# Differential attention scores: the low-part term of the keys over 128 rows in place of 64, with keys doubled by a DMA

## The chip, the cores and the metric

The kernel runs on one core of a Trainium2 chip. The metric is the time of one execution on the device in microseconds, as the median of several runs. The engines are TensorE (PE for its matmuls, PEld for its weight loads), VectorE (DVE), ScalarE (ACT), GpSimd (POOL) and SyncE (SP, whose queue issues the DMAs here).

## The reference

One block of a transformer on a sequence of 512 tokens of width 2048, in float32. Branch A is differential attention with 8 heads: each head has two queries and two keys of 64 columns, two softmaxes, and one value of 128 columns. Branch B is grouped-query attention with 8 heads of 128 columns.

```
h = rmsnorm(x, norm_g); proj = h @ w_in            # (512, 10752)
qa, ka, va, za, qb, kb, vb, zb, ga, gb = split(proj)
# branch A, per head, with 1-D rope on q and k:
s1 = q1 @ k1.T * 64 ** -0.5;  s2 = q2 @ k2.T * 64 ** -0.5
p  = softmax(s1) - lam * softmax(s2)
oa = rmsnorm(p @ v, subln_g) * (1 - lam_init)
ya = (oa * silu(za)) @ w_out_a
# branch B: rmsnorm of q and k, axial rope, softmax, 4 query heads to a key head
yb = (ob * silu(zb)) @ w_out_b
x  = x + (sigmoid(ga) * ya + sigmoid(gb) * yb) @ w_o
out = rmsnorm(x, final_g)
```

## The kernel before, in words

Each float32 product is made of float32r products: an operand is split into a rounded high part and the remaining low part, and hi·hi, lo·hi and hi·lo are added up in PSUM. The split is `hi_lo` (lines 102 to 104): ScalarE casts the high part, VectorE subtracts it.

The kernel has three stages. First the norm of x and most of the input projection, with all gates, in Strassen's form (line 234). Then the sixteen heads of attention, between whose steps TensorE takes pieces of plain products, called fills (`stream_steps`, line 175): what is left of the input projection, then the output projection of branch B, and at the end that of branch A. Then the rest of the output projections, the merge and the final norm.

The order of the heads is the list `HEADS` (B0 B1 A0 B2 B3 B4 B5 A1 A2 B6 B7 A3 A4 A5 A6 A7), and `FILLS` gives for each head how many fills follow its first two score tiles, its last two, and the turning of its probabilities. On TensorE that order is the order of the program (`manual_schedule`); on the other engines, and in SP's queue of DMAs, a scheduler orders the instructions by its own estimates. So the order of those changes with the program.

The loop over heads issues for head n: `scores(0)`, `scores(1)`, the attention product of the head before (`finish`, line 618), fills, `scores(2)`, `scores(3)`, then `turn` of head n+1 (its operands for the scores), `prepare` of head n+2 (loads and rope), `norm` of the head before (lines 685 and 686), fills, `turn_p` (16 transposes of the probabilities, line 605), fills.

A head of branch A holds its two halves on the partitions: rows 0 to 63 of the turned queries and keys are the first half, rows 64 to 127 the second. `turn` makes for each half a tile `qs` of 128 rows, [q_hi; q_lo], and a tile `kh` of 128 rows, [k_hi; k_hi]: four casts of 64 rows on ScalarE (line 643), as a half has to reach both halves of the partitions. The low part `kl` is one tile of 128 rows for both halves (lines 637 and 638). A score tile of one half is then two matmuls of 512 columns, line 660 over all 128 rows (q_hi·k_hi + q_lo·k_hi) and line 661 over the 64 rows of its half (q_hi·k_lo):

```
for half in range(2):
    qs, kh, src = self.ops[half]
    sp = aux()
    nc.tensor.matmul(out=sp, lhsT=qs[:, sl], rhs=kh, start=True, stop=False)
    nc.tensor.matmul(out=sp, lhsT=qs[src, sl], rhs=self.kl[src], start=False, stop=True)
```

A call of `scores(i)` does this for two halves, and two calls stand together, so that TensorE takes blocks of eight matmuls, lines 660 and 661 in turn: 2 blocks for each of 8 heads, 16 in all. The softmax after each tile is a maximum on VectorE (`nmax`, line 576), an exponential on ScalarE (line 579), a scaling on ScalarE (line 668) and the combination of both halves into `p` on VectorE (line 669). Branch B's score tiles are three matmuls over 128 rows each (line 735).

Of the kernel before, what the change touches and what calls it, by code (L numbers as in the profile page):

```python
# [17 lines left out]
P = 128  # L18
# [12 lines left out]
# blocks of 128 columns of the intermediate that keeps the branches' projections  # L31
# [6 lines left out]
# which of them take Strassen's form, four at a time, and which are taken plainly beside the heads  # L38
# [3 lines left out]
# heads of branch B whose scalings ScalarE does  # L42
WIDE = "0125"
# halves of tiles of w whose products go before the first head and between the steps of each
# [5 lines left out]
def hybrid_block_kernel(  # L50
# [5 lines left out]
    """Every float32 product runs as three single-pass float32r products: each operand is split  # L56
    exactly into a rounded high part and the remaining low part (hi*hi + lo*hi + hi*lo). All but
    the keys and queries of branch A and the branches' output projections take Winograd's form of Strassen's product (seven eighths of the work)."""
# [4 lines left out]
    # the eight banks of PSUM, shared between accumulators and the rest  # L63
# [33 lines left out]
    def rsqrt_pool(dst, ss, mul, add, n):  # L97
        """dst = (ss * mul + add) ** -0.5 on a few columns."""
        nc.gpsimd.tensor_scalar(out=dst, in0=ss, scalar1=mul, scalar2=add, op0=ALU.mult, op1=ALU.add)
        nc.gpsimd.tensor_tensor(out=dst, in0=dst, in1=neg_half[:, :n], op=ALU.pow)  # L100
# [12 lines left out]
    def split_w(raw, free=None):  # L113
        """free: a raw slot from which the parts' places may be taken, with its next."""
# [9 lines left out]
    def load_w(w, pieces, kc, step):  # L124
        """Rows kc * 128.. of some columns of w, [128, step, columns]."""
# [11 lines left out]
    def stream_steps(w, pieces, nk, natural, act, done, order=None, early=None, halves=False):  # L137
        """Products with some columns of w (512 or 256, made of `pieces` of columns), over nk
        contraction tiles, in banks of PSUM [128, 512].
        natural: tokens by columns, act(k, t).T @ w; done(first token tile, bank), the token tiles of  # L140
        a bank side by side. Else columns by tokens, w[:, c].T @ act(k); done(c, bank). halves: so, but
        one half of the tokens after the other, act(k, half).
        A generator, of two steps for each tile of w."""
# [4 lines left out]
        # of a product: its bank, its place there, the columns of w, what act takes, first and last of the bank  # L148
# [12 lines left out]
        # two tiles of w take turns where the halves of the tokens do  # L161
# [24 lines left out]
    def strassen(w, c_left, c_right, act, natural, tmp, done, tail=None, before={}):  # L186
        """Winograd's form of Strassen's product over the whole contraction (2048 rows of w, its
        upper and lower 1024) for 256 + 256 columns of w and the two halves of the tokens.
        act: the seven sums of quarters of the activations, each [128, 8, 256], split hi/lo.
        tmp(): a [128, 2, 256] tile; done(token half, column half, psum, sbuf): a result, the sum of  # L190
        the two, [128, 2, 256]. natural: rows of the results are tokens, else columns of w. tail:
        the first half of the tokens comes early and the last results by token tiles; tail(u, p5, t)
        takes what the results have before: both of the other half, its right one alone and the right one
        of the first half. before:
        what prepares a sum of act, by its name."""
# [79 lines left out]
        # the next group's quarters take the slots in the order in which they fall free  # L275
# [13 lines left out]
    # the halves of the width, [128, token half, contraction tile, 256], hi and lo  # L289
# [9 lines left out]
    def keep_cols(blocks, t0, nt, v):  # L299
        """Token tiles t0.. of some 128-column blocks of the projection, [128, nt, columns], to DRAM."""  # L300
        for i, b in enumerate(blocks):
            written[b] = written.get(b, 0) + nt
            nc.sync.dma_start(out=pv[b, :, t0:t0 + nt, :], in_=v[:, :, i * P:(i + 1) * P])
# [10 lines left out]
    def plain_cols(blocks, place, **kw):  # L314
        """Blocks of 128 columns of the projection by tokens, as they come, kept in DRAM."""
# [9 lines left out]
    def plain_rows(blocks, place, **kw):  # L325
        """The same the other way: columns by tokens."""
# [12 lines left out]
    with tc.tile_pool(name="xs", bufs=1) as xs:  # L339
        # ---- h = rmsnorm(x), transposed: its quarters (halves of the tokens and of the width) and  # L340
        # ---- their sums; the first product needs the quarters alone
# [3 lines left out]
        with tc.tile_pool(name="xn", bufs=1) as xn:  # L345
            # the gain, by channels on the partitions
# [28 lines left out]
            def turned_in(kp):  # L375
                """Where the transposed quarters of two contraction tiles stay for a while, in the
                place of what they come from: [128, token half, tile, width half, 256]."""
# [50 lines left out]
            # ---- the other columns of branches A and B, kept in DRAM  # L428
# [9 lines left out]
            # the first ones go beside the last sums of quarters; results go where these were, the first  # L438
            # of them after a while in PSUM
# [639 lines left out]
```

## Time and profile before

| | |
|---|---|
| median of 3 runs | 1399.37 us (1399.13, 1399.37, 1401.01) |
| profiled execution | span 1399.1 us from its first to its last instruction; no other time is given for it, and the fastest run, 1399.13 us, is the same to the last digit |
| PE busy | 1375.2 us, 98% of the span |
| PEld, DVE, ACT, POOL busy | 1272.8, 1081.0, 720.0, 85.8 us |
| DMA | 200.02 MB, mean 143 GB/s |
| attention stage | from about 735 to 1143 us of the span |

In a timeline each row is the start in us, the length in us, the engine, the line, the operation and its output and inputs. Matmuls overlap: the length of one is from its start to its modelled end, so what one costs in a row of them is read from the starts, not from the lengths. In brackets stand the idle time before an instruction and what ended it. "64\*128 64x512" is a matmul over 64 rows with 512 columns. PEclk in a table of windows is the granted share of TensorE's full clock.

### The profile page before, as it was taken

How to read it: one execution, taken by the hardware profiler on the slowest of the kernel's cores; microseconds unless marked ns; L12 is line 12 of the kernel's file. 1: busy time of each engine (PE TensorE's matmuls, PEld its weight loads, DVE VectorE, ACT ScalarE, POOL GpSimd, SP SyncE). 2: the span in 40 equal slices, each digit the busy share in tenths (PEclk: the TensorE clock that was granted, in tenths of full speed). 3: DMA queues.
4: the chain of work that ended last, by engine and by line, in shares of the span. 5: the costliest groups of instructions: out<-in, count | busy, mean ns of one | idle time of the engine just before them, and what ended most of it. 6: DMA issues, size and time to landing. Idle time of an engine off the chain costs nothing.

```text
span 1399.1 us, 24056 instructions
## 1 busy us (share of the span) xinstructions
PE 1375.2 (98%) x9625; PEld 1272.8 (91%) x9625; DVE 1081.0 (77%) x1392; ACT 720.0 (51%) x1134; POOL 85.8 (6%) x94
## 2 busy tenths in 40 slices
PE   6999999999999999999999999999999999999997
PEld 5999999999999999999998798778777778899997
DVE  5967777777777877777758778677788867899986
ACT  7643334444444444444457667665766753444444
POOL 1000000000000000000021010000000010004322
PEclk9999999999999999999999999999999999999999
DMA  8245444544334344443366344435565336563333
GB/s 286 87 134 172 124 124 120 151 151 144 115 119 129 119 132 151 144 134 119 125 200 181 107 144 143 123 111 158 153 180 160 117 111 211 175 230 112 99 103 120
DMA packets 199183, 200.02 MB, mean 143 GB/s; under 512 B 10768, under 2 KB 174880, under 8 KB 198432
## 3 DMA queue, kind: packets, MB, share of 16 engines
q1 hardware_dynamic: 199072, 198.49, 45.7%
q8 instruction: 75, 1.23, 0.4%
q14 instruction: 36, 0.29, 0.1%
HBM read 165.68 MB, written 32.77 MB: 142 GB/s over the span
## 4 chain that ended last, share of the span: by engine, by line
PE 94%; DVE 2%; ACT 1%; issue 1%; DMA 0%; POOL 0%; SPq 0%; POOLq 0%; DVEq 0%; ACTq 0%
PE acc L234 55%; PE acc L175 28%; PE aux L618 3%; PE aux L605 2%; PE aux L661 2%; PE aux L660 2%; PE aux L735 2%; DVE w_lo L104 1%; DVE w_raw L209 1%; DMA xt<-in_x_dram 0%; PE aux L389 0%; PE aux L587 0%; ACT sq L366 0%; ACT w_hi L103 0%; PE aux L685 0%
## 5 line engine op out<-in xcount | busy, mean ns | idle before, releaser
L103 ACT CAST w_hi<-w_raw 128x1024 fp32r<-128x1024 f32 x351 | 368.5, 1050 | 517.0 <-PE acc L234 397.7
L104 DVE TENSOR_TENSOR w_lo<-w_raw,w_hi 128x1024 fp32r<-128x1024 f32 x351 | 434.5, 1239 | 166.2 <-ACT w_hi L103 163.6
L209 DVE TENSOR_TENSOR w_raw<-w_raw 128x1024 f32<-128x1024 f32 x160 | 200.0, 1250 | 2.4
L234 PE MATMUL acc<-a2l,w_hi 128*128 128x256 f32 x384 | 108.7, 283 | 0.0
L234 PE MATMUL acc<-a2h,w_hi 128*128 128x256 f32 x384 | 108.7, 283 | 0.0
L234 PE MATMUL acc<-a2h,w_lo 128*128 128x256 f32 x384 | 108.7, 283 | 0.0
L576 DVE TENSOR_REDUCE nmax<-aux 128x1 f32<-128x512 f32 x96 | 64.5, 687 | 17.5 <-PE aux L661 15.0
L234 PEld LDWEIGHTS acc<-a2h,w_hi 128*128 128x128 f32 x384 | 73.7, 192 | 0.0
L234 PEld LDWEIGHTS acc<-a2l,w_hi 128*128 128x128 f32 x384 | 73.7, 192 | 0.0
L234 PEld LDWEIGHTS acc<-a2h,w_lo 128*128 128x128 f32 x384 | 73.7, 192 | 0.0
L175 PE MATMUL acc<-a1h,w_hi 128*128 128x512 f32 (+1 forms) x160 | 56.4, 357 | 0.2 <-ACT a1h L393 0.2
L175 PE MATMUL acc<-a2h,w_hi 128*128 128x512 f32 (+1 forms) x160 | 55.5, 350 | 0.0
L175 PE MATMUL acc<-a2l,w_hi 128*128 128x512 f32 (+1 forms) x160 | 55.5, 348 | 0.0
L175 PE MATMUL acc<-a1h,w_lo 128*128 128x512 f32 (+1 forms) x160 | 55.4, 351 | 0.0
L175 PE MATMUL acc<-a2h,w_lo 128*128 128x512 f32 (+1 forms) x160 | 55.4, 347 | 0.0
L175 PE MATMUL acc<-a1l,w_hi 128*128 128x512 f32 (+1 forms) x160 | 55.2, 350 | 0.1
L234 PE MATMUL acc<-s1h,w_lo 128*128 128x256 f32 x192 | 54.3, 283 | 0.0
L234 PE MATMUL acc<-s4h,w_lo 128*128 128x256 f32 x192 | 54.3, 283 | 0.0
L234 PE MATMUL acc<-s1h,w_hi 128*128 128x256 f32 x192 | 54.3, 283 | 0.0
L234 PE MATMUL acc<-s1l,w_hi 128*128 128x256 f32 x192 | 54.3, 283 | 0.0
L234 PE MATMUL acc<-s2h,w_lo 128*128 128x256 f32 x192 | 54.3, 283 | 0.0
L234 PE MATMUL acc<-a1h,w_hi 128*128 128x256 f32 x192 | 54.3, 283 | 0.0
(326 smaller groups left out, 4376.9 us busy)
## 6 DMA issues: line engine op xcount, KB each, us to landing
w_raw<-in_w_in_dram SPq DMA_DIRECT2D x136, 512.0 KB, 3.5
w_raw<-in_w_in_dram SPq DMA_DIRECT2D x64, 256.0 KB, 3.6
w_raw<-in_w_o_dram SPq DMA_DIRECT2D x32, 512.0 KB, 4.0
gg<-kept SPq DMA_DIRECT2D x32, 256.0 KB, 2.5
w_raw<-in_w_out_b_dram SPq DMA_DIRECT2D x32, 256.0 KB, 3.2
rows<-gg SPq DMA_DIRECT2D x32, 256.0 KB, 3.1
w_raw<-in_w_out_a_dram SPq DMA_DIRECT2D x32, 256.0 KB, 3.3
cols<-pv SPq DMA_DIRECT2D x26, 256.0 KB, 2.9
```

Of the source, the lines that this page charges most:

```text
L103: nc.scalar.copy(out=hi, in_=src)
L104: nc.vector.tensor_tensor(out=lo, in0=src, in1=hi.bitcast(F32), op=ALU.subtract)
L175: nc.tensor.matmul(out=acc[b][:, place], lhsT=l, rhs=r, start=first and kc == order[0] and k == 0 and i == 0, stop=last and kc == order[-1 ...
L209: nc.vector.tensor_tensor(out=d, in0=u, in1=v, op=ALU.subtract)
L234: nc.tensor.matmul(out=ps[u] if by_row else ps[:, u, :], lhsT=l, rhs=r, start=n % (2 if by_row else 4) == 0 and k == 0 and i == 0, stop=n ...
L576: nc.vector.tensor_reduce(out=nmax, in_=sps, axis=AX.X, op=ALU.max, negate=True)
L605: nc.tensor.transpose(out=tp[:, i * P:(i + 1) * P], in_=self.p[i][:, j * P:(j + 1) * P], identity=ident)
L618: nc.tensor.matmul(out=o, lhsT=l, rhs=r, start=j == 0 and i == 0, stop=j == NT - 1 and i == 2)
L660: nc.tensor.matmul(out=sp, lhsT=qs[:, sl], rhs=kh, start=True, stop=False)
L661: nc.tensor.matmul(out=sp, lhsT=qs[src, sl], rhs=self.kl[src], start=False, stop=True)
L735: nc.tensor.matmul(out=sp, lhsT=l, rhs=r, start=n == 0, stop=n == 2)
```

## The change

Line 661's product runs over all 128 rows, [q_hi; q_lo] against [k_lo; k_lo], so each half gets a `kl` of its own with the low part on both halves of the partitions; the term q_lo·k_lo is added by it. The doubling moves from casts to DMAs: a new step `double()` copies each half of the roped keys twice, SBUF to SBUF, into a tile `kd` (4 DMAs of 64 rows and 128 KB for a head, 32 in all), and `turn` makes `kh` and `kl` from `kd` by `hi_lo`, 128 rows at a time. `double()` of head n+1 is called at the start of head n. `kn` goes, `kd` has four buffers (two tiles of two), `kl` now takes two buffers for a head. To make room, `y1` of the norm shares the place of `sqh`, and `bsq` of branch B's norm has a place of its own.

```
     class Head:
+        def double(self):
+            pass
...
     class HeadA(Head):
+        def double(self):
+            self.kd = [at.tile([P, S], F32, name="kd", tag="kd", bufs=2) for _ in range(2)]
+            for half in range(2):
+                for d in range(2):
+                    nc.sync.dma_start(out=self.kd[half][d * 64:d * 64 + 64], in_=self.k[half * 64:half * 64 + 64])
+
         def turn(self):
-            k, q = self.k, self.q
-            kl = at.tile([P, S], F32R, name="kl", tag="kl")
-            kh = [at.tile([P, S], F32R, name="kh", tag="kh") for _ in range(2)]
+            q = self.q
             self.ops = []
-            kn = at.tile([P, S], F32R, name="kn", tag="kn", bufs=1)
-            nc.scalar.copy(out=kn, in_=k)
-            nc.vector.tensor_tensor(out=kl, in0=k, in1=kn.bitcast(F32), op=ALU.subtract)
             for half in range(2):
                 src, oth = slice(half * 64, half * 64 + 64), slice(64 - half * 64, P - half * 64)
+                kh = at.tile([P, S], F32R, name="kh", tag="kh")
+                kl = at.tile([P, S], F32R, name="kl", tag="kl")
+                hi_lo(kh, kl, self.kd[half])
                 qs = at.tile([P, S], F32R, name="qs", tag="qs")
-                for d in (src, oth):
-                    nc.scalar.copy(out=kh[half][d], in_=k[src])
                 nc.scalar.mul(out=qs[src], in_=q[src], mul=0.125)
...
-                self.ops.append((qs, kh[half], src))
-            self.kl = kl
+                self.ops.append((qs, kh, kl))
...
-                qs, kh, src = self.ops[half]
+                qs, kh, kl = self.ops[half]
                 sp = aux()
                 nc.tensor.matmul(out=sp, lhsT=qs[:, sl], rhs=kh, start=True, stop=False)
-                nc.tensor.matmul(out=sp, lhsT=qs[src, sl], rhs=self.kl[src], start=False, stop=True)
+                nc.tensor.matmul(out=sp, lhsT=qs[:, sl], rhs=kl, start=False, stop=True)
...
-        sq = at.tile([P, P], F32, name="bsq", tag="y1", bufs=1)
+        sq = at.tile([P, P], F32, name="bsq", tag="bsq", bufs=1)
...
-            y1 = at.tile([P, S], F32, name="y1", tag="y1", bufs=1)
+            y1 = at.tile([P, S], F32, name="y1", tag="sqh", bufs=1)
...
         heads[1].prepare()
+        heads[0].double()
         fill(FILL_FIRST)
...
             last = heads[n - 1] if n else None
+            if n + 1 < len(heads):
+                heads[n + 1].double()
             head.scores(0)
```

TensorE's own order stays the same, matmul for matmul. On VectorE the order between the maxima of head A6's last two score tiles and its last `p` (where A7 is turned) was this:

```order
L576 TENSOR_REDUCE nmax<-aux 128x1 x4
L666 RECIPROCAL rs<-ssum 128x2
L104 TENSOR_TENSOR w_lo<-w_raw,w_hi 128x1024
L667 TENSOR_SCALAR rs<-rs,nlam 128x1
L669 SCALAR_TENSOR_TENSOR p<-e_12036,rs,p 128x512
L666 RECIPROCAL rs<-ssum 128x2
L798 TENSOR_TENSOR rows<-acc,rows 128x512
L667 TENSOR_SCALAR rs<-rs,nlam 128x1
L669 SCALAR_TENSOR_TENSOR p<-e_12056,rs,p 128x512
L645 SCALAR_TENSOR_TENSOR qs<-cols,qs 64x512
```

In the changed kernel it is this:

```order
L576 TENSOR_REDUCE nmax<-aux 128x1 x4
L670 RECIPROCAL rs<-ssum 128x2
L104 TENSOR_TENSOR kl<-kd,kh 128x512
L671 TENSOR_SCALAR rs<-rs,nlam 128x1
L104 TENSOR_TENSOR w_lo<-w_raw,w_hi 128x1024
L673 SCALAR_TENSOR_TENSOR p<-e_12070,rs,p 128x512
L670 RECIPROCAL rs<-ssum 128x2
L650 SCALAR_TENSOR_TENSOR qs<-cols,qs 64x512
L671 TENSOR_SCALAR rs<-rs,nlam 128x1
L104 TENSOR_TENSOR kl<-kd,kh 128x512
L673 SCALAR_TENSOR_TENSOR p<-e_12090,rs,p 128x512
L650 SCALAR_TENSOR_TENSOR qs<-cols,qs 64x512
```

Two `kl` and one `qs` of A7 now stand ahead of A6's last `p`, and the `rows` (a result of a fill, read out of its PSUM bank) that stood ahead of it comes after.

On ScalarE the same place began with the first cast of A7's `kh`, from the keys in `cols`, and two more instructions of A7 stood within the exponentials and scalings:

```order
L643 CAST kh<-cols 64x512
L579 ACTIVATE p,ssum<-aux,nmax 128x512
L579 ACTIVATE e_12036,ssum<-aux,nmax 128x512
L579 ACTIVATE p,ssum<-aux,nmax 128x512
L668 ACTIVATE p<-p,rs 128x512
L579 ACTIVATE e_12056,ssum<-aux,nmax 128x512
L643 CAST kh<-cols 64x512
L668 ACTIVATE p<-p,rs 128x512
L644 ACTIVATE qs<-cols 64x512
L643 CAST kh<-cols 64x512 x2
L644 ACTIVATE qs<-cols 64x512
```

Now the first cast reads `kd`, which a DMA fills:

```order
L103 CAST kh<-kd 128x512
L579 ACTIVATE p,ssum<-aux,nmax 128x512
L579 ACTIVATE e_12070,ssum<-aux,nmax 128x512
L579 ACTIVATE p,ssum<-aux,nmax 128x512
L672 ACTIVATE p<-p,rs 128x512
L579 ACTIVATE e_12090,ssum<-aux,nmax 128x512
L649 ACTIVATE qs<-cols 64x512
L103 CAST kh<-kd 128x512
L672 ACTIVATE p<-p,rs 128x512
L649 ACTIVATE qs<-cols 64x512
```

The first cast still stands ahead of the four exponentials. Behind the last exponential two instructions of A7 instead of one stand ahead of the last scaling, and one instead of four behind it.

In SP's queue, where A7's four DMAs of `kd` went in, the order was first this (`gg`, `yg` are intermediates in DRAM, `w_raw` a tile of weights):

```order
L525 DMA rows<-gg 128x512 x2
L130 DMA w_raw<-in_w_out_a_dram 128x2x256 x3
L799 DMA yg<-rows 128x512
L130 DMA w_raw<-in_w_out_a_dram 128x2x256
L525 DMA rows<-gg 128x512
```

and is now this:

```order
L525 DMA rows<-gg 128x512 x2
L637 DMA kd<-cols 64x512 x2
L130 DMA w_raw<-in_w_out_a_dram 128x2x256 x2
L637 DMA kd<-cols 64x512 x2
L130 DMA w_raw<-in_w_out_a_dram 128x2x256 x2
L803 DMA yg<-rows 128x512
```

Each pair of copies stands ahead of two loads of weights.

## Rows read from the trace of the kernel before

**Rows 1.** The page: span, busy time, and the chain that ended last by engine.

```profile
span 1399.1 us, 24056 instructions
PE 1375.2 (98%) x9625; PEld 1272.8 (91%) x9625; DVE 1081.0 (77%) x1392; ACT 720.0 (51%) x1134; POOL 85.8 (6%) x94
...
PE 94%; DVE 2%; ACT 1%; issue 1%; DMA 0%; POOL 0%; SPq 0%; POOLq 0%; DVEq 0%; ACTq 0%
```

**Rows 2.** Windows: us; busy PE, PEld, DVE, ACT, POOL; PEclk, DMA share, GB/s.

```profile
735.00:1145.00 410.00, 410.00 (x1938) 324.04 (x1938) 319.64 (x576) 275.79 (x559) 23.98 (x21) 0.99 0.47 142
```

**Rows 3.** Lines 660 and 661, PE: ns min/median/max, first and last start, forms.

```profile
L660 PE MATMUL aux<-kh,qs x64: 392/495/502, 785.5 to 1123.6; 128*128 128x512 f32 x64
...
L661 PE MATMUL aux<-kl,qs x64: 492/498/501, 785.8 to 1124.0; 64*128 64x512 f32 x64
```

**Rows 4.** Timeline of PE: first block of eight matmuls, then A6's second.

```profile
785.46 0.39 PE L660 MATMUL aux<-kh,qs 128*128 128x512 f32 x1
...
788.77 0.50 PE L618 MATMUL aux<-ph,vbh 128*128 128x512 f32 x1
789.11 0.40 PE L618 MATMUL aux<-ph,vbl 128*128 128x512 f32 x1
...
1092.95 0.39 PE L660 MATMUL aux<-kh,qs 128*128 128x512 f32 x1
1093.28 0.50 PE L661 MATMUL aux<-kl,qs 64*128 64x512 f32 x1
1093.70 0.49 PE L660 MATMUL aux<-kh,qs 128*128 128x512 f32 x1
...
1096.27 0.50 PE L685 MATMUL aux<-sqh,ones 128*128 128x512 f32 x1
...
1102.28 1.91 PE L605 MATMUL aux<-ident,p 128*128 128x128 f32 x16
```

**Rows 5.** Timeline of PE: branch B's scores, and a fill with one operand held twice.

```profile
761.89 0.39 PE L735 MATMUL aux<-kbh,qh 128*128 128x512 f32 x1
...
763.26 0.39 PE L618 MATMUL aux<-ph,vbh 128*128 128x512 f32 x1
...
735.89 0.28 PE L175 MATMUL acc<-w_hi,a2h 128*128 128x256 f32 x1
736.01 0.28 PE L175 MATMUL acc<-w_lo,a2h 128*128 128x256 f32 x1
736.13 0.28 PE L175 MATMUL acc<-w_hi,a2l 128*128 128x256 f32 x1
```

**Rows 6.** PE's clock: a window, and the timeline behind another block of eight.

```profile
921.00:924.00 3.00, 3.00 (x8) 2.32 (x7) 2.52 (x6) 1.78 (x5) 0.00 (x0) 0.50 0.09 26
...
1002.46 0.63 PE L175 MATMUL acc<-og1h,w_hi 128*128 128x512 f32 x1
...
1005.88 0.49 PE L175 MATMUL acc<-og1l,w_hi 128*128 128x512 f32 x1
```

**Rows 7.** Lines 643 and 638: casts of `kh`, subtraction of `kl`.

```profile
L643 ACT CAST kh<-cols x32: 612/618/626, 754.4 to 1101.6; 64x512 fp32r<-64x512 f32 x32
...
L638 DVE TENSOR_TENSOR kl<-cols,kn x8: 670/680/683, 753.1 to 1070.2; 128x512 fp32r<-128x512 f32 x8
```

**Rows 8.** Timeline of DVE and ACT at A6's last two score tiles.

```profile
1096.37 0.69 DVE L576 TENSOR_REDUCE nmax<-aux 128x1 f32<-128x512 f32 x1 [0.17 <-PE aux L661]
...
1100.67 0.75 DVE L669 SCALAR_TENSOR_TENSOR p<-e,rs,p 128x512 f32<-128x512 f32 x1
...
1095.08 0.62 ACT L643 CAST kh<-cols 64x512 fp32r<-64x512 f32 x1 [0.88 <-PE aux L660]
```

**Rows 9.** SP's queue where A7's copies go in, and DMAs of 128 KB.

```profile
1067.43 1.62 SPq L525 DMA_DIRECT2D rows<-gg  x2
1070.26 0.90 SPq L130 DMA_DIRECT2D w_raw<-in_w_out_a_dram  x2
...
pv<-kept SPq DMA_DIRECT2D x24, 128.0 KB, 1.9
```

## The prediction

> **What bounds the kernel now.** I read the page first: TensorE is busy for 1375.2 of 1399.1 us, and the chain that ended last is TensorE's for 94% of the span [rows 1]. The change lies in the attention stage, so its window comes next: from 735 to 1145 us TensorE has no idle time at all, VectorE is busy for 319.6 of 410 us and ScalarE for 275.8 [rows 2]. What shortens TensorE's row of work there shortens the kernel, as long as the other two, which supply each step's operands, keep up.
>
> Busy is not full speed, though, so I read the two lines that the change touches and then the starts of their matmuls. Lines 660 and 661 have 64 matmuls each, alike in columns; one has 128 rows and the other 64 [rows 3]. In the first block of eight the first starts at 785.46 and the matmul behind the block at 788.77 [rows 4]: 3.31 us, or 0.41 us for one. Within a block the first step is 0.33 us and the others 0.42 to 0.43 [rows 4]. Branch B's scores have the same columns, but 128 rows throughout: six take 763.26 − 761.89 = 1.37 us, 0.228 for one [rows 5]. So alternating between the two forms costs about 0.2 us at each step, on the engine that sets the end.
>
> **The change, part by part.** *Matmuls.* None is added or taken away; 64 of them go from 64 to 128 rows. I count nine steps for a block, as the one behind it is late too: 789.11 − 785.46 = 3.65 us [rows 4]. Nine steps at branch B's pace are 9 × 0.228 = 2.05 us [rows 5]. That saves 1.60 us for a block, and 16 × 1.60 = 25.6 us in all. One doubt is that both matmuls of a pair now hold the same `qs` one after the other, which branch B's do not. A fill does that: the two matmuls that hold `a2h` in a row start at 735.89 and 736.01 and the next at 736.13, an even 0.12 us for 256 columns [rows 5]. So I take the full 25.6; the bounds are nothing, if the late step is due to something else that stays, and 25.6.
>
> *The clock.* Twice in this stage the granted clock falls to half, from 2.4 to 1.2 GHz: a window at 921 us shows 0.50 [rows 6]. Both times it falls where a block of eight ends; the second time eight matmuls behind the block take 1005.88 − 1002.46 = 3.42 us [rows 6] instead of 8 × 0.228 = 1.82. That is 1.6 us lost each time, 3.2 together. In the other 14 blocks it does not fall. With the blocks' slow steps gone, I expect the falls to go as well: −3.2 us, with 0 as the other bound if they go elsewhere.
>
> *ScalarE.* It loses 32 casts of `kh` and 8 of `kn` and gets 16 casts of 128 rows: 24 fewer at 0.62 us [rows 7] are 14.9 us of work. The engine is not the bound, so I count nothing for it but room.
>
> *VectorE.* There are 8 more subtractions for `kl` at 0.68 us [rows 7], 5.4 us over a stage in which it idles for 90 [rows 2]. They hide there, except where they stand on the way from a score tile to `turn_p`. At A6, which I take as the tight case, the last `p` ends at 1100.67 + 0.75 = 1101.42 [rows 8] and the transposes that need it start at 1102.28 [rows 4]: 0.86 us of slack. After the change TensorE comes there 1.60 us earlier. The chain behind the scores gets shorter too, as the maxima now wait for TensorE: the last of them idled 0.17 us for its matmul [rows 8], and scores that come 0.23 instead of 0.43 us apart take this wait from all four, about 0.7 us. Against that, two `kl` and a `qs` now stand ahead of the last `p` and one `rows` moves behind it: two instructions more, some 1.3 us by 0.68 each [rows 7]. Some of it falls where VectorE would have waited for ScalarE anyway, whose first cast of `kh` need no longer wait until 1095.08 [rows 8] but comes about 1 us sooner after the block's start. I set the shortfall at 0.3 us for a head, 8 × 0.3 = 2.4 us in all. The bounds are 0 and, if nothing of the chain got shorter and 1.3 us came on top, 1.60 + 1.3 − 0.86 = 2.0 us a head, 16 us.
>
> *DMAs.* 32 copies within SBUF come in, which the trace does not show in that form. The nearest rows are stores of 128 KB, which land in 1.9 us [rows 9]. A7's copies stand in SP's queue behind the two loads of `gg` at 1067.43 and ahead of the loads of weights at 1070.26 [rows 9]. They are wanted at A7's first cast, at 1095.08 in the old time [rows 8]. Even if each pair waits some 5 us for A6's `turn` to release its buffers, and holds the loads of weights behind it for as long, the copies have some 18 us of cover. So I count them at nothing. Without that cover they would cost what the slower rival below says. Less than nothing is excluded, as they take no work from TensorE.
>
> *Places.* `y1` in the place of `sqh` waits for both matmuls that read `sqh`, which it needs anyway for the mean; `bsq` no longer waits for `y1`. Both count as nothing.
>
> *Sum.* 1399.1 − 25.6 − 3.2 + 2.4 = 1372.7 us for the profiled execution, which is 0.3 us below the median of the runs; against that median, **1373.0 us**.
>
> **A rule that speaks against the change.** The rows say that a pair over 64 and 128 rows is slower than one over 128 alone [rows 4, 5]. The Trainium skill's page "TensorE: Matmul & The Clock Gate", in its section "Why this matters for your kernels", says that one matmul with a small contraction takes as long as one with 128 rows, and that smaller ones gain only when several run side by side. By that rule alone the wider product would be worth nothing and the sum would stay at 1399; this trace does not agree, for 0.41 us against 0.228 is the price of mixing the forms in one row of work, of which the rule does not speak. What it would mean here is the second rival.
>
> **The rivals.** *First, the softmax chain becomes the bound* in branch A's heads. For it: the slack at A6 is 0.86 us against a TensorE 1.60 us faster, and VectorE gets work in that very place. Against it: VectorE idles for 22% of the stage [rows 2] and ScalarE loses 14.9 us. If the eight heads each give back between the 0.3 us of my sum and the bound of 2.0, say 1.2, the time is 1373.0 + 8 × 0.9 = 1380; at the bound it is 1373.0 + 13.6 = 1387.
>
> *Second, the step of 0.42 us stays*, because it belongs to these operands and not to the number of rows; it decides if eight matmuls over 128 rows of `qs` still take over 3 us. Then the clock stays too, and only the 2.4 us of VectorE come: about 1400 to 1402. Against it stand branch B's six matmuls and the fill [rows 5].
>
> *Third, the other side: the copies come late.* On ScalarE the cast of `kh` stands ahead of the four exponentials, so a `kd` that has not landed holds the whole softmax of the running head, and with it `turn_p`, in each of eight heads. The gain of 25.6 + 3.2 − 2.4 = 26.4 us is 3.3 us for a head. From the point where a copy lands more than 3.3 us after the cast could have run, plus any slack, the kernel is slower than before: at 5 us late the time is 1373.0 + 8 × 5 = 1413. That takes a copy that lands over 20 us behind its place in the queue, where 128 KB land in 1.9 [rows 9].
>
> **How the numbers follow.** A measurement of this kernel can tell about 0.2%, 2.8 us, from no change. I give my forecast (blocks at full pace, small shortfalls, falls of the clock gone or partly so) 0.66; the softmax chain as the new bound 0.23; the step that stays 0.05; late copies on the slower side 0.04; and 0.02 to something in which little moves. The first two are faster by far more than 2.8 us. The step that stays lies within or just past the 0.2%, and I count it and the rest as no change, 0.07; so slower keeps 0.04 and faster 0.89. The range goes from 1368, if neither the chain nor the clock costs anything and the new order of the queues brings a little (1399.4 − 25.6 − 3.2 = 1370.6 is the sum without a shortfall), to 1387, the first rival at its bound. It leaves out the last three cases.
>
> **What would show it.** In the profile after, a block of eight should take 1.8 us from its first start to the matmul behind it, with no form of 64 rows on TensorE; if it takes over 3, the second rival holds. The window of the stage should end some 26 us earlier, with PEclk at 1.00. Idle time of TensorE ahead of `turn_p`, ended by `p`, measures my 2.4 us: 8 us or more of it mean the first rival. ScalarE's first cast of `kh` should be ended by TensorE, as now, and never by a DMA; waits for `kd` there mean the third. I am wrong if the stage is not shorter, or if what it gains is lost again behind 1143 us, in the products that follow.

## The result, and the profile after

The changed kernel takes 1377.28 us (median of four runs, 1375.15 to 1378.63), the kernel before 1399.89 (four runs, 1399.13 to 1401.01): a ratio of 0.9832, with a 95% interval of 0.9818 to 0.9846. It is faster by 1.7%. The forecast was 1373.0 us with a range of 1368 to 1387, and 0.89 on faster.

The page of the changed kernel: span, busy times, and the chain that ended last by engine.

```profile
span 1374.9 us, 24100 instructions
PE 1350.2 (98%) x9625; PEld 1274.1 (93%) x9625; DVE 1081.1 (79%) x1400; ACT 702.9 (51%) x1110; POOL 84.5 (6%) x94
PE 90%; DVE 4%; ACT 2%; DMA 1%; issue 1%; POOL 0%; SPq 0%; DVEq 0%; POOLq 0%; ACTq 0%
```

Beside [rows 1] the span is 24.2 us shorter, and TensorE's busy time falls by 25.0 us with the same 9625 matmuls. ScalarE loses 17.1 us, VectorE gains 0.1. TensorE's share of the chain falls from 94% to 90%, and VectorE, ScalarE and a DMA take over what it lost: TensorE now waits in some places.

The two lines of branch A's scores in the changed kernel (duration in ns as minimum, median and maximum; first and last start; form), where [rows 3] had two forms:

```profile
L664 PE MATMUL aux<-kh,qs x64: 389/389/393, 786.8 to 1099.5; 128*128 128x512 f32 x64
...
L665 PE MATMUL aux<-kl,qs x64: 389/389/398, 787.0 to 1099.8; 128*128 128x512 f32 x64
```

TensorE's timeline in the changed kernel: the first block of eight, A6's second block with the matmul behind it, and the places where TensorE waited. The idle time in brackets counts from the modelled end of the matmul before, so what a wait costs is taken below from the starts, and is more.

```profile
786.78 0.39 PE L664 MATMUL aux<-kh,qs 128*128 128x512 f32 x1
787.01 0.39 PE L665 MATMUL aux<-kl,qs 128*128 128x512 f32 x1
...
788.60 0.39 PE L621 MATMUL aux<-ph,vbh 128*128 128x512 f32 x1
...
860.63 1.64 PE L608 MATMUL aux<-ident,p 128*128 128x128 f32 x13 [0.49 <-DVE p L555]
...
988.61 0.50 PE L175 MATMUL acc<-og1l,w_hi 128*128 128x512 f32 x1 [0.18 <-DVE og1l L104]
...
994.87 0.50 PE L175 MATMUL acc<-og1h,w_hi 128*128 128x512 f32 x1 [0.51 <-ACT og1h L103]
...
1072.76 0.39 PE L664 MATMUL aux<-kh,qs 128*128 128x512 f32 x1
...
1074.58 0.39 PE L689 MATMUL aux<-sqh,ones 128*128 128x512 f32 x1
...
1081.14 1.64 PE L608 MATMUL aux<-ident,p 128*128 128x128 f32 x13 [0.17 <-DVE p L673]
```

A block takes 788.60 − 786.78 = 1.82 us, and 1074.58 − 1072.76 = 1.82 at A6, where [rows 4] show 3.31 and 3.32. All 16 blocks take 1.82 to 1.84. The step behind a block is no longer late either: 0.227 us instead of 0.338 where no fall of the clock adds to it (0.108 instead of 0.165 behind the two blocks that transposes follow).

TensorE's weight loads show where the 0.2 us of a step lay. First the loads and a matmul of the kernel before, then a load of the changed one:

```profile
785.23 0.19 PEld L660 LDWEIGHTS aux<-kh,qs 128*128 128x128 f32 x1
785.78 0.18 PEld L661 LDWEIGHTS aux<-kl,qs 64*128 64x128 f32 x1 [0.36 <-issue]
785.78 0.50 PE L661 MATMUL aux<-kl,qs 64*128 64x512 f32 x1
...
786.78 0.19 PEld L665 LDWEIGHTS aux<-kl,qs 128*128 128x128 f32 x1
```

Among equal forms the weights of a matmul are loaded while the one before it runs: from 785.23 for the matmul at 785.46 [rows 4], and from 786.78 for the one at 787.01. At the change of form in the kernel before, the load begins only with its own matmul, at 785.78, and so it is at every change of that block. A load takes 0.18 to 0.19 us, about the price of a change.

Windows of the changed kernel (us; busy PE, PEld, DVE, ACT, POOL; PEclk, DMA share, GB/s): the attention stage, the 7 us ahead of it, and its first 7 us.

```profile
735.00:1120.00 385.00, 383.50 (x1935) 324.11 (x1935) 318.40 (x584) 258.39 (x534) 23.91 (x21) 1.00 0.54 162
728.00:735.00 7.00, 5.16 (x43) 4.87 (x42) 6.37 (x16) 4.04 (x11) 6.16 (x10) 0.98 0.62 183
735.00:742.00 7.00, 7.00 (x48) 7.00 (x48) 7.00 (x11) 2.51 (x8) 0.00 (x0) 0.77 0.67 195
```

The two falls of the clock of [rows 6] are gone. A new one stands at the start of the stage: 0.77 is the mean over 7 us of a stretch at half the clock and one at the full clock. In the same 7 us the kernel before had the full clock throughout, though TensorE had idled about as much ahead of them (busy for 5.00 of the 7 us there, 5.16 here):

```profile
735.00:742.00 7.00, 7.00 (x55) 6.74 (x55) 7.00 (x11) 1.37 (x4) 0.00 (x0) 1.00 0.78 213
```

**Where the time went.** TensorE does the same work in the same order, so its row can be laid beside the old one piece by piece. Its last operation of the stage starts at 1118.54 instead of 1143.09 us, 24.55 us sooner. The 16 blocks with the late steps behind them give 25.5 us (16 × 1.49 + 14 × 0.11 + 2 × 0.06). The two falls of the clock give 1.64 + 1.60 = 3.2, and the new one takes 1.3 back. Waits take 3.0 by the starts, at three places: 0.72 us at B4's `turn_p`, 0.54 + 1.27 at two runs of fills of A3, and 0.45 at A6's `turn_p`. That sums to −24.4; the other 0.15 us are small pieces.

VectorE and ScalarE show what is late at these places: B4's last `p`, A3's gated output `og1h` with the `kl` behind it, and A6's last `p`.

```profile
858.30 1.22 DVE L104 TENSOR_TENSOR w_lo<-w_raw,w_hi 128x1024 fp32r<-128x1024 f32 x1
...
860.10 0.48 DVE L555 TENSOR_SCALAR p<-p,rs 128x512 f32<-128x512 f32 x1
...
990.31 0.62 ACT L103 CAST kh<-kd 128x512 fp32r<-128x512 f32 x1 [0.91 <-PE aux L664]
...
992.34 0.62 ACT L103 CAST og1h<-rows 128x512 fp32r<-128x512 f32 x1 [0.37 <-DMA rows<-og]
...
994.42 0.67 DVE L104 TENSOR_TENSOR kl<-kd,kh 128x512 fp32r<-128x512 f32 x1
...
1079.74 0.68 DVE L104 TENSOR_TENSOR kl<-kd,kh 128x512 fp32r<-128x512 f32 x1
1080.35 0.74 DVE L673 SCALAR_TENSOR_TENSOR p<-e,rs,p 128x512 f32<-128x512 f32 x1
```

At B4 a subtraction of weights (1.22 us) stands ahead of the last `p`. At A3 the load of the gated output, its cast and its subtraction are a chain of their own, `rows<-og` to `og1h` to `og1l`, with the head's exponentials and a `kl` on the two engines between. At A6 it is the predicted case: a `kl` just ahead of the last `p`.

The copies of the keys, by their issues (KB each, median us from issue to landing), and the longest waits of SP's queue at their line:

```profile
kd<-cols SPq DMA_DIRECT2D x32, 128.0 KB, 2.4
...
SPq L637 <- DVE kl L104: 8.3, 6, 2.9
```

They land in 2.4 us, where the nearest rows had shown 1.9 [rows 9]. SP stands 8.3 us in all for a buffer of theirs, 2.9 at the longest. Where ScalarE idles ahead of a cast of `kh`, TensorE ends the wait, never a DMA.

### The profile page after: what moved, and what is told of

Its sections match the earlier page's. It is cut to its first block, busy times and chain, and to the rows that moved or that the text cites. A ratio compares the mean times of both kernels' runs of the same rounds, so it can differ in the third digit from the quotient of the medians.

```text
span 1374.9 us, 24100 instructions
## 1 busy us (share of the span) xinstructions
PE 1350.2 (98%) x9625; PEld 1274.1 (93%) x9625; DVE 1081.1 (79%) x1400; ACT 702.9 (51%) x1110; POOL 84.5 (6%) x94
## 4 chain that ended last, share of the span: by engine, by line
PE 90%; DVE 4%; ACT 2%; DMA 1%; issue 1%; POOL 0%; SPq 0%; DVEq 0%; POOLq 0%; ACTq 0%
PE acc L234 55%; PE acc L175 27%; PE aux L621 3%; PE aux L608 2%; PE aux L739 1%; DVE w_lo L104 1%; PE aux L664 1%; PE aux L665 1%; DVE w_raw L209 1%; DMA rows<-og 1%; DMA xt<-in_x_dram 1%; PE aux L389 0%; DMA rows<-yg 0%; ACT sq L366 0%; ACT w_hi L103 0%
## 5 line engine op out<-in xcount | busy, mean ns | idle before, releaser
L576 DVE TENSOR_REDUCE nmax<-aux 128x1 f32<-128x512 f32 x96 | 61.0, 681 | 7.5 <-PE aux L739 4.7
L234 PE MATMUL acc<-a1l,w_hi 128*128 128x256 f32 x192 | 54.3, 283 | 0.0
L234 PE MATMUL acc<-a1h,w_lo 128*128 128x256 f32 x192 | 54.3, 283 | 0.0
```

Of the source, the lines that this page charges most:

```text
L234: nc.tensor.matmul(out=ps[u] if by_row else ps[:, u, :], lhsT=l, rhs=r, start=n % (2 if by_row else 4) == 0 and k == 0 and i == 0, stop=n ...
L576: nc.vector.tensor_reduce(out=nmax, in_=sps, axis=AX.X, op=ALU.max, negate=True)
```

## The experiments

The theory: TensorE pays about 0.2 us whenever it goes from 128 rows to 64 or back; the gain is that price and nothing else, and the rest of the change matters only by what it puts on the other engines. The rivals: the gain is from fewer casts, or from the new orders of the queues; the price belongs to something else in these operands; the copies or the softmax hold back a larger gain. The runs stand in the order of the argument, not of their numbers. Ratios are against the kernel before, run beside each experiment on the same chip; its medians there were 1402.38 us for e1, e2, e3 and e5 and 1402.74 for e4 and e6 to e8, so times of different comparisons aren't set against each other more finely than that. e9 and e10 have one run each, and the argument takes from them the rows of their traces.

**e1: the changed kernel with 64 rows again.**

```
-                nc.tensor.matmul(out=sp, lhsT=qs[:, sl], rhs=kl, start=False, stop=True)
+                src = slice(half * 64, half * 64 + 64)
+                nc.tensor.matmul(out=sp, lhsT=qs[src, sl], rhs=kl[src], start=False, stop=True)
```

> The changed kernel with one part undone: the keys are still doubled by DMAs and both tiles kl are still made, but the second matmul of each pair runs over the 64 rows of its half again (the term q_lo*k_lo is left out, as before the change). Theory (the gain is on TensorE, in the blocks that mixed 64 and 128 rows): a block of eight takes 3.3 us again, and of the gain of about 23 us nearly all is lost, 1398 to 1402 us, perhaps 1 to 3 us above the kernel before for the extra work on VectorE. Rival (the gain comes from the casts that left ScalarE and from the new order): 1376 to 1380 us.

Measured: 1402.18 us, ratio 1.000 [0.9988, 1.0013]. Timeline of TensorE, first block and what follows it, and B4's `turn_p`:

```profile
787.50 0.39 PE L664 MATMUL aux<-kh,qs 128*128 128x512 f32 x1
787.82 0.50 PE L666 MATMUL aux<-kl,qs 64*128 64x512 f32 x1
...
790.81 0.50 PE L621 MATMUL aux<-ph,vbh 128*128 128x512 f32 x1
...
864.75 1.42 PE L608 MATMUL aux<-ident,p 128*128 128x128 f32 x11 [0.72 <-DVE p L555]
```

The blocks are back at 3.31 us and the whole gain is lost, though the copies, the fewer casts and the new orders all stay. So these bring nothing by themselves. On every engine the order of e1's instructions is that of the changed kernel. Its waits at A3 and A6 are gone all the same, so they need a TensorE that arrives sooner; B4's stays, so it came from VectorE's new order.

**e2: the kernel before, its matmuls grouped by form.** In a block the four of 128 rows come first and then the four of 64, halves in turn; no keys are doubled.

```
-            for half in range(2):
-                qs, kh, src = self.ops[half]
-                sp = aux()
+            todo = [(j, half, slice(j * P, (j + 1) * P), aux()) for j in (i, i + 1) for half in range(2)]
+            for j, half, sl, sp in todo:
+                qs, kh, src = self.ops[half]
                 nc.tensor.matmul(out=sp, lhsT=qs[:, sl], rhs=kh, start=True, stop=False)
+            for n in (0, 1, 2, 3):
+                j, half, sl, sp = todo[n]
+                qs, kh, src = self.ops[half]
                 nc.tensor.matmul(out=sp, lhsT=qs[src, sl], rhs=self.kl[src], start=False, stop=True)
```

> The kernel before the change, with the eight matmuls of a block in another order: first the four over 128 rows, then the four over 64 rows, the two halves of the rows in turn. Theory A (a change between 128 and 64 rows costs about 0.2 us, and nothing else does): two changes a block instead of eight, a block of 8 x 0.228 + 2 x 0.2 = 2.2 us, 16 x 1.2 = 19 us gained, 1380 us. Theory B (a matmul over 64 rows costs 0.4 us more by itself, whatever stands beside it): a block stays at 3.3 us, 1400 us. Theory C (as A, and two matmuls on different halves of the rows also run side by side): 4 x 0.228 + 2 x 0.228 + 0.4 = 1.8 us, 1376 us.

Measured: 1379.97 us, ratio 0.9835 [0.9817, 0.9853]. Timeline of TensorE (x4 and x2: rows drawn together; the third and fourth rows are the same four matmuls in narrower stretches, by pairs):

```profile
787.34 1.07 PE L661 MATMUL aux<-kh,qs 128*128 128x512 f32 x4
788.34 0.73 PE L665 MATMUL aux<-kl,qs 64*128 64x512 f32 x4
...
788.34 0.50 PE L665 MATMUL aux<-kl,qs 64*128 64x512 f32 x2
...
788.68 0.40 PE L665 MATMUL aux<-kl,qs 64*128 64x512 f32 x2
...
789.00 0.50 PE L618 MATMUL aux<-ph,vbh 128*128 128x512 f32 x1
789.34 0.39 PE L618 MATMUL aux<-ph,vbl 128*128 128x512 f32 x1
```

A block takes 1.66 us and the step behind it 0.34: 2.00 for nine, against 2.05 after the change. Putting equal forms together wins what the change wins, without a wider product. Theory C comes out: the four of 64 rows take 0.66 us in all and start as two pairs, 0.34 us apart. Its 1.8 us count both changes of form in full, but 0.11 us of the second shows in the step behind the block; nine matmuls are then 7 × 0.228 + 2 × 0.2 = 2.00. In time e2 doesn't get ahead of the change, because its trace has other losses: TensorE waits for A6's last `p`, and the clock is at half behind that wait (timeline and window of e2):

```profile
1082.77 2.28 PE L605 MATMUL aux<-ident,p 128*128 128x128 f32 x13 [2.36 <-DVE p L678]
...
1084.00:1087.00 3.00, 3.00 (x11) 2.51 (x11) 3.00 (x6) 1.86 (x4) 0.00 (x0) 0.50 0.50 163
```

Whether that wait can be had back was not tried.

**e3: the same, with the two of one half next to each other.**

```
-            for n in (0, 1, 2, 3):
+            for n in (0, 2, 1, 3):
```

> As the run before it, but of the four matmuls over 64 rows the two on the lower half of the rows stand together and then the two on the upper half. Theory A: 2.2 us a block as there, 1380 us. Theory B: 3.3 us, 1400 us. Theory C: slower than the run before it by one step of 0.228 us a block, as only the pair in the middle lies on different halves: some 4 us more, 1380 us.

Measured: 1379.50 us, ratio 0.9834 [0.9819, 0.9850], blocks of 1.67 us. The difference that Theory C wanted isn't there: the trace shows the same two pairs. Its rows don't name the half of a matmul, but the semaphore updates recorded with the matmuls give a sign. In ten of the 16 blocks one of the four updates none, which fits only the second in the program: VectorE takes its maximum after that of the third and so needs no signal of its own. The one without an update starts third. So the pairs there are most likely still of one matmul from each half, started in another order than the program's; no run shows it directly.

**e9: grouped, with all four of 64 rows on rows 0 to 63.**

```
-                nc.tensor.matmul(out=sp, lhsT=qs[src, sl], rhs=self.kl[src], start=False, stop=True)
+                nc.tensor.matmul(out=sp, lhsT=qs[0:64, sl], rhs=self.kl[0:64], start=False, stop=True)
```

> The grouped kernel again, but all four matmuls of 64 rows take rows 0 to 63 of their operands, so none of them works on the other half of the partitions (the second half's low term is therefore formed from the wrong rows, and its value differs). In the grouped kernel's trace the four matmuls of 64 rows start as two pairs, 788.34 and 788.68, with two starts within 0.01 us. Theory P: two that lie on different halves run side by side, and that is why four take 0.66 us. Then here there are no pairs: starts 0.228 us apart or more, the four take 0.9 to 1.0 us, a block 1.9 to 2.0 us, and the profiled span is 16 x 0.3 = 4 to 6 us above the 1378.5 of the grouped kernel. Theory Q: matmuls of 64 rows in a row are shorter by themselves; then the starts and the block of 1.66 us stay.

Measured, one run: 1385.17 us beside 1401.67 of the kernel before, span 1383.4. Timeline of TensorE:

```profile
786.08 1.07 PE L661 MATMUL aux<-kh,qs 128*128 128x512 f32 x4
787.08 1.20 PE L665 MATMUL aux<-kl,qs 64*128 64x512 f32 x4
788.21 0.50 PE L618 MATMUL aux<-ph,vbh 128*128 128x512 f32 x1
788.55 0.40 PE L618 MATMUL aux<-ph,vbl 128*128 128x512 f32 x1
```

This is Theory P, with more time than it gave (0.9 to 1.0 us, 1.9 to 2.0 for the block), as parts of both changes lie in it: without a partner on the other half the four take 1.13 us instead of 0.66, and the block 2.13. This also gives the price without a count of steps: nine take 788.55 − 786.08 = 2.47 us, 0.42 more than 9 × 0.228, for two changes of form: 0.21 each. In the kernel before nine take 3.65, 1.60 more, for eight changes: 0.20 each.

**e10: the kernel before, its 64 rows always on rows 0 to 63.** The edit is e9's, made in the kernel before.

> The kernel before, matmuls in turn as there, but every matmul of 64 rows takes rows 0 to 63, for both halves (the second half's low term is formed from the wrong rows). Theory A: the price of 0.2 us a step belongs to the change between 128 and 64 rows, whichever half they lie on. Then a block stays at 3.31 us and the time that of the kernel before. Rival: the price belongs to going from one half of the partitions to the other; then the blocks lose some of it and take 1.8 to 2.6 us, and the time falls by 16 x 0.7 to 16 x 1.5 us, 11 to 24 us.

Measured, one run: 1399.24 us beside 1401.67. Timeline of TensorE:

```profile
787.18 0.39 PE L660 MATMUL aux<-kh,qs 128*128 128x512 f32 x1
787.50 0.50 PE L661 MATMUL aux<-kl,qs 64*128 64x512 f32 x1
...
790.49 0.50 PE L618 MATMUL aux<-ph,vbh 128*128 128x512 f32 x1
```

The block is 3.31 us, and so are all 16: the price is for the change of row count, not of the half. Instruction for instruction its order is that of the kernel before, on every engine. In its trace the stage ends 1.74 us sooner all the same, and the pieces that differ are the clock's: the two falls of [rows 6] are not there (−1.6 each), and one at the start of the stage is (+1.5). Windows of e10, the start of the stage and the two places of [rows 6]:

```profile
735.00:742.00 7.00, 7.00 (x48) 7.00 (x47) 7.00 (x11) 1.48 (x3) 0.06 (x1) 0.76 0.73 205
915.00:930.00 15.00, 15.00 (x56) 10.04 (x55) 10.49 (x19) 8.47 (x17) 0.00 (x0) 1.00 0.40 123
1000.00:1010.00 10.00, 10.00 (x39) 7.28 (x40) 8.67 (x17) 8.62 (x18) 0.00 (x0) 1.00 0.37 106
```

**e4: the copies in GpSimd's queue.**

```
-                    nc.sync.dma_start(out=self.kd[half][d * 64:d * 64 + 64], in_=self.k[half * 64:half * 64 + 64])
+                    nc.gpsimd.dma_start(out=self.kd[half][d * 64:d * 64 + 64], in_=self.k[half * 64:half * 64 + 64])
```

> The changed kernel with the 32 copies of kd issued by GpSimd's queue in place of SP's. Theory (TensorE's wait at A3, 1.8 us, is the chain that loads and splits the gated outputs, which TensorE now reaches sooner; the copies do not cause it): the wait stays between 1 and 2.5 us, and the time within 1 us of the changed kernel's, 1376 to 1378 us. Rival (the copies hold up SP's queue, and with it the loads of gated outputs): the wait at A3 is gone, 1374 to 1376 us. B4's 0.7 us at turn_p should stay under both.

Measured: 1377.43 us, ratio 0.9826 [0.9809, 0.9843], against the change's 0.9832. SP's queue is rid of all 32 issues and of their waits, and nothing comes of it. In its trace A3's second wait is gone and the first is 0.52 us in brackets, 0.9 by the starts. That is half of the 1.8 and less than the theory's 1 to 2.5 us, so the copies or the order that came with them have a part in A3's wait. But B4's stays (0.66 us in brackets), A6's too (0.17), and the norm of A0 and a later transpose lose 1.1 and 0.45 us by the starts: the waits move with the order.

**e5: doubled by casts, without copies.** `kh` and `kl` are made 64 rows at a time, both halves of each.

```
-                hi_lo(kh, kl, self.kd[half])
+                for d in (src, oth):
+                    nc.scalar.copy(out=kh[d], in_=self.k[src])
+                    nc.vector.tensor_tensor(out=kl[d], in0=self.k[src], in1=kh[src].bitcast(F32), op=ALU.subtract)
```

> The changed kernel with the doubling by the engines in place of the DMAs: four casts of 64 rows a head on ScalarE for kh (as before the change) and four subtractions of 64 rows on VectorE for kl, no kd. Theory (the matmuls make the gain; the doubling matters only by what stands ahead of p): blocks of 1.82 us as in the changed kernel; ScalarE gets 2 casts and VectorE 2 subtractions more a head, some 1.3 us each in the chain to turn_p, so up to 8 x 1.3 = 10 us of stalls: 1377 to 1387 us, likely 1381. Rival (the DMAs in the queue of SP hold up loads of weights and of gated outputs, and the stalls come from there): faster than the changed kernel, 1373 to 1375 us.

Measured: 1379.33 us, ratio 0.9833 [0.9815, 0.9851]. ScalarE is busy for 714.0 us and VectorE for 1092.4, 11 us more each than in the changed kernel, and the ratio is the same. All blocks but one (2.77 us) take 1.82. TensorE's waits stand elsewhere. The longest, 1.44 us, is in branch B at 966 us; two more from its timeline:

```profile
1004.52 0.50 PE L175 MATMUL acc<-og1h,w_hi 128*128 128x512 f32 x1 [1.06 <-DVE rows L801]
...
1085.26 1.64 PE L608 MATMUL aux<-ident,p 128*128 128x128 f32 x13 [0.54 <-DVE p L672]
```

**e6: fills moved to the three places that wait.**

```
-FILLS = "141 141 131 131 030 021 032 142 121 350 121 131 332 331 222 232".split()
+FILLS = "141 141 131 131 030 030 032 142 121 350 121 041 332 331 132 232".split()
```

> The changed kernel with three fills moved behind the last two score tiles, so that the softmax has more cover before turn_p: B4 021 to 030, A3 131 to 041, A6 222 to 132. Theory (the three places where TensorE waits, 3.0 us in all, are the softmax chain at B4 and A6 and the gated outputs at A3, each short of cover): B4's 0.7 and A6's 0.45 us go, A3's 1.8 us shrinks, no new wait over 0.5 us: 1374 to 1376 us. Rival (each fill moved opens the same wait at the place that it came from): 1377 to 1379 us.

Measured: 1376.95 us, ratio 0.9821 [0.9804, 0.9837]: not to be told from the change. B4's `turn_p` no longer waits, but the fill that A6 gave up is missed at the norm ahead of it, and A3's gated output stays late:

```profile
994.46 0.50 PE L175 MATMUL acc<-og1h,w_hi 128*128 128x512 f32 x1 [0.38 <-ACT og1h L103]
...
1072.52 0.50 PE L689 MATMUL aux<-sqh,ones 128*128 128x512 f32 x1 [1.10 <-ACT sqh L103]
```

**e7: the softmax first.** The maxima, exponentials, scalings and `p` of all heads get the scheduler's high priority.

```
-                softmax_exp(sp, e, ssum[:, half:half + 1])
+                with tc.high_priority():
+                    softmax_exp(sp, e, ssum[:, half:half + 1])
```

> The changed kernel with a high priority for the softmax (maxima, exponentials, scaling, p), so that the scheduler puts p ahead of the second kl at A6. Theory (kl and qs of the next head, which the change put ahead of the last p, make the waits at B4 and A6): both waits at turn_p go, 1.2 us, 1375 to 1377 us; A3's 1.8 us stays, as it comes from the gated outputs. Rival (the waits are only TensorE's faster pace): B4 and A6 stay as they are, 1377 us.

Measured: 1382.40 us, ratio 0.9859 [0.9844, 0.9874]: slower than e4 and e6 (1377.43 and 1376.95), which were measured together with it. B4's and A6's `turn_p` wait no more, as the theory of the softmax chain wants, but the gated output of A3 pays for it:

```profile
990.07 0.50 PE L175 MATMUL acc<-og1h,w_hi 128*128 128x512 f32 x1 [2.67 <-ACT og1h L103]
...
997.66 0.50 PE L175 MATMUL acc<-og1h,w_hi 128*128 128x512 f32 x1 [1.67 <-ACT og1h L103]
```

**e8: e6 and e7 together.** Both edits as above.

> The two runs before it together. Theory: no wait of TensorE over 0.3 us between 740 and 1120 us but at A3, 1374 to 1376 us. Rival (the moves undo each other): as the changed kernel, 1377 us or more.

Measured: 1386.58 us, ratio 0.9888 [0.9873, 0.9903]. TensorE waits six times in A3's fills, 2.8 us in all for `og1h` and as much for `og1l`, and the granted clock is 0.50 from 1002.5 to 1009 us there. Waits of 0.44 us elsewhere, too, are more than its theory allowed. The two edits don't add.

No variant is clearly faster than the changed kernel: the ratios of e2 to e6 lie between 0.9821 and 0.9835, and its own is 0.9832.

## Why the prediction was right, and where it was not

**Matmuls: right, in place and size.** 25.6 us were predicted for the blocks, 25.5 came. The doubt, two matmuls with the same `qs` in a row, is void: the steps are 0.23 us. e1 shows that without the wider form nothing of the gain is left, e2 that an end to the mixing is enough for it, and e10 that the half plays no part in the price. The prediction put the price on each of nine steps; e9 shows that it belongs to each change of form, 0.2 us, eight of them in a block before.

**The second rival (the step stays): fell.** The rows of e2 and e9 also settle the rule that was weighed. By the Trainium skill's "TensorE: Matmul & The Clock Gate", "Why this matters for your kernels", a small contraction gains only where several run side by side. The rows agree as far as it goes: on one half, four of 64 rows are no cheaper than four of 128 (1.13 us, the changes' price partly in it, against 4 × 0.228 = 0.91); in pairs they take 0.66. For the price of mixing, another page of the Trainium skill, "TensorEngine Tiling (Array Packing)", "Key Properties", states that changing the mode in which the array is divided drains TensorE. That fits the weight loads above, which at a change don't run ahead; that a slice of 64 rows is such a change of mode is an inference. The page gives no figure; here it is 0.2 us.

**The clock: the sum nearly, the reason not.** The two falls went, as forecast, but not because the slow steps went: e1 and e10 keep these steps, and in both traces the falls are gone. And a fall came at the start of the stage that the sum did not have, 1.3 us; e10 shows it with the instructions of the kernel before in their order, where the trace of before has none. So a fall that costs 1.3 to 1.6 us comes and goes with the execution. The runs of the kernel before show the same without a trace: in 13 of them on one chip the mean granted clock went from 0.993 to 0.998 and the span from 1403.5 to 1397.0 us, the shortest span at the highest clock. What decides it stays open; e2, e3, e7, e8 and e9 each have a fall behind a wait of TensorE, between 1.5 and 2.7 us long, but the falls of the kernel before have no wait ahead of them. The term was −3.2; these two traces give −3.2 + 1.3 = −1.9, and of a gain against a median of runs it was no safe part.

**VectorE's shortfall: nearly right in size, wrong in place.** 2.4 us were spread over eight heads; 3.0 came, at three. A6 waited for its last `p`, by 0.45 us where 0.3 was taken for a head. B4's 0.72 is of branch B, which the prediction did not look at: there the scheduler put a subtraction of weights ahead of the last `p`, which in the kernel before stood behind it. A3's 1.8 us, the largest, are a wait for the gated output. The prediction followed only the way from a score tile to `turn_p` and so missed it: a TensorE that is 1.6 us sooner at each block is sooner at the fills too, and their operands come by a chain of a load, a cast and a subtraction; by e4 the new queue order has a part in it.

**First rival: fell, with its mechanism seen at A6 alone.** e7 shows that putting the softmax first doesn't free the time but moves the wait to the fills, at a loss.

**DMAs and the third rival: right at nothing.** No cast waited for a copy, and e4 took the copies out of SP's queue without an effect on the time that can be measured. **Places and ScalarE: right at nothing.** e1 has all of it, the new places, the fewer casts and the copies, and takes the time of the kernel before; e5 gives ScalarE and VectorE 11 us more work each, and the ratio doesn't move.

**The sum.** 1372.7 us were worked out for the profiled execution, whose span is 1374.9. Of the 2.2 us the new fall of the clock is 1.3, the larger waits 0.6, and small pieces, most of them behind the stage, the rest. The median of the runs then stands 2.4 us above that span, where 0.3 was allowed, and here a step failed that has nothing to do with the change: the execution before was given its span, 1399.1 us, as its time. In the profiled run of the changed kernel the time is 1.8 us above the span (1376.67 beside 1374.9). By that distance, the profiled execution before took some 1400.9 us (an estimate) and stood 1.5 above the median of 1399.37, not 0.3 below it. It held two falls of the clock, and losses of a slower execution cannot be won back from the median: the traces differ by 24.2 us, the medians by 22.6. The forecast of 1373.0 us was missed by 4.3: 2.2 are the pieces above, and 2.1 this step.

## What to carry to other kernels

On a TensorE that sets the end, look at the starts of matmuls, not at their busy time: matmuls over 64 rows between matmuls over 128 cost 0.2 us at every change here (512 columns, float32r), so group equal forms or pad the small ones, whichever is cheaper on the other engines; here both give the same time. Where grouping puts the 64-row matmuls of both halves together, they run in pairs, which saves 0.47 us for four (2.13 against 1.66) and pays for the two changes. When a bound engine gets faster by a piece, list what feeds each of its next operations, the fills as well as the step in hand: the largest new wait was in a chain that the change did not touch.

## What the runs showed of the hardware that was not expected

- Two 64-row matmuls on different halves of the partitions start together (788.34 in e2, two starts) and the next two 0.34 us later; on one half the four take 1.13 us in place of 0.66 (e9).
- At a change between 128 and 64 rows the weights are loaded only as their matmul starts (785.78 for both in the kernel before), among equal forms 0.23 us ahead (785.23 for 785.46).
- A change between 128 and 64 rows costs 0.20 to 0.21 us (1.60 us for eight, 0.42 for two), whichever half the 64 rows lie on.
- The granted clock was 0.76 over the first 7 us of the stage in e10 and 1.00 at both places of [rows 6], with the kernel before's own order of instructions; and 13 runs of the kernel before itself had a mean clock of 0.993 to 0.998: those falls are of an execution, not of the blocks.
